# A hybrid decoder block on one core: 160 gathered tokens and 352 dense ones instead of 128 and 384

## The chip, the core and the metric

The program runs on one core of one Trainium2 chip. The metric is the device time of one execution in microseconds. A Trainium2 core has a matrix engine (TensorE, PE in the rows, with its weight loads as PEld), a vector engine (DVE), a scalar engine (ACT), a general engine (GpSimd, POOL) and a queue engine (SyncE, SP). Each engine runs its own instructions in order; 16 DMA engines move data between memory and the on-chip buffer of 128 partitions.

## What is computed

512 tokens of 2048 channels and 16 learned tokens ahead of them go through two mixers side by side (a convolution and a gated linear attention), a residual, and a mixture of 16384 tiny experts ("PEER"). The change is in the last part alone:

```python
def _peer(xn, wq, k1, k2, U, V):            # 8 heads, 128 keys, top 16
    q = (xn @ wq).reshape(B, L, 8, 256)
    s1 = einsum('blhd,hnd->blhn', q[..., :128], k1)
    s2 = einsum('blhd,hnd->blhn', q[..., 128:], k2)
    v1, i1 = top_k(s1, 16); v2, i2 = top_k(s2, 16)
    cand, cidx = v1[..., :, None] + v2[..., None, :], i1[..., :, None] * 128 + i2[..., None, :]
    top_s, pos = top_k(cand, 16)
    idx, gate = cidx[pos], softmax(top_s)   # 8 * 16 = 128 experts of each token
    h = gelu(einsum('thkd,td->thk', U[idx], x))
    return einsum('thk,thkd->td', gate * h, V[idx])
...
h = h + mixed @ w_out
h = h + _peer(rmsnorm(h, norm2_g), ...)
return rmsnorm(h, normf_g)[:, 16:]
```

U and V have 16384 rows of 2048 fp32 numbers, 8 KB a row. Each token uses 128 of them.

## The kernel before

The experts are computed in two ways. The first 128 tokens are **gathered**: a token lies on each partition, and for each of its 128 slots one indirect DMA (`_gather`, L711, issued by POOL at L713) brings 128 rows, one a partition, 1 MB, into a buffer `rows`, of which there are two. For the rows of U, DVE multiplies them with the token and sums (L731, result in a column of `gw`); for those of V, it adds them, times a weight, to `ytok` (L746). That is 256 gathers, the 128 of U first. The other 384 tokens (`TD`) are **dense**: TensorE multiplies them with all 16384 rows of U and V, each fp32 number split into a high and a low part, in three products (L87, L89, L91 for U; L873 to L875 for V), and the gate of an expert that a token did not choose is zero. A weight tile of 1 MB is loaded by SP into `raw` (two buffers), ACT writes its high half `whi` (L68) and DVE the low half `wlo` (L71), in two halves of 1024 columns, of which three buffers each exist.

After the mixers (the first 2050 us of the span) the program runs in these stages:

- the choice (`_select`, to 2309 us): queries, scores, top 16, with the tokens' rows (`_token_rows`, `xtok`, L702) and the dense tokens' normed columns (`_dense_row`, tile `dnh`, four buffers, loaded by POOL's queue at L578). DVE has nearly all of it. In this stage POOL also computes `wlo`.
- B, 2310 to 2850 us: the tiles of U from 8 to 60 (128 experts a tile, 48 matmuls of 384 columns, `_up_tile`), whose results go to memory (`hlag`). Beside each tile stands a step of `_gate_steps`, which makes the dense gates by one-hot products, 8 tokens at a time (48 such steps): DVE compares (`b` L774, `a` L776), POOL and ACT multiply (`ag`), TensorE multiplies (`pg`), ACT and DVE write them out (`stage`, L795). One gather follows each tile.
- D, 2877 to 3373 us: groups 0 to 6 of the second product. A group is 1024 experts; it has four quarters of the output's channels, each two tiles of V and 96 matmuls. After each quarter `gather(2)`. `_w_piece` loads gates (`gt`, L842) and hidden values (`gel`, L848) through POOL's queue and multiplies them on DVE (L851, L509).
- E, 3373 to 4446 us: groups 7 to 14, each quarter followed by two more tiles of U for the next group, and the gathers that are left (147) shared evenly over 96 places, three in a quarter. A quarter here is 192 matmuls and four weight tiles.
- the last group, 4446 to 4521 us, in which `_Final` finishes the gathered tokens: it transposes `ytok`, adds the residual `hg` (L971), squares and sums (L974), scales and stores them, while the last experts of the others run; then 19 us for the norm of the dense tokens.

The list of gathers is one queue (`gsteps`); `gather(n)` takes the next n. Each engine's order is fixed by a scheduler when the program is built: what stands under `high_priority` (weights, `_w_piece`, sums into `yT` at L882) goes ahead, and a gather is issued no earlier than the last `wlo` emitted before it. The gather's DVE step stands in DVE's one queue among the `wlo` that TensorE needs next.

Of the kernel before, what the change touches and what calls it, by code (L numbers as in the profile page):

```python
# [698 lines left out]
def _token_rows(g, sp):
    """The normed rows of the first TG tokens, token on partition."""  # L700
    nc = g.nc
    nc.gpsimd.tensor_tensor(g.xtok.rearrange("p (c t) -> p c t", t=TG), _bf(g.x2h[:, :, :TG]), _bf(g.x2l[:, :, :TG]), op=OP.add)  # L702
    for c in range(4):
        cs = slice(c * 512, (c + 1) * 512)
        ps = g.p2.tile([P, 512], F32, tag="ps2", name="ps2")
        for j in range(4):
            _transpose(nc, ps[:, j * P:(j + 1) * P], g.xtok[:, c * 512 + j * P:c * 512 + (j + 1) * P], g.ident)
        nc.scalar.activation(g.xtok[:, cs], ps, AF.Copy, scale=g.rc[:, :1])


def _gather(g, rows, src, col):  # L711
# [7 lines left out]
def _gather_steps(g):  # L719
    """The experts of the first TG tokens, row by row: one closure per gathered set of rows."""  # L720
    nc, a = g.nc, g.a
    st = Ctx()

    def up(s):
        def f():
            if s == 0:
                st.h = g.gp.tile([P, SLOTS], F32, name="ghd")
                st.w = g.gp.tile([P, SLOTS], F32, name="gw")
            rows = g.rp.tile([P, D], F32, tag="rows", name="rows", bufs=2)
            _gather(g, rows, a["un"], s)  # L730
            nc.vector.scalar_tensor_tensor(rows, rows, 1.0, g.xtok, op0=OP.mult, op1=OP.mult, accum_out=st.h[:, s:s + 1])  # L731
            if s % TOPK == TOPK - 1:
                hs = slice(s + 1 - TOPK, s + 1)
                nc.scalar.activation(st.w[:, hs], st.h[:, hs], AF.Gelu)
                nc.vector.tensor_tensor(st.w[:, hs], st.w[:, hs], g.gate[:, 0, hs], op=OP.mult)
        return f

    def down(s):
        def f():
            rows = g.rp.tile([P, D], F32, tag="rows", name="rows", bufs=2)  # L740
            _gather(g, rows, a["vn"], s)
            if s == 0:
                g.ytok = g.gp.tile([P, D], F32, tag="xtok", name="ytok", bufs=1)
# [409 lines left out]
```

## Time and profile before

| | us |
|---|---|
| median of 3 runs | 4539.19 |
| lowest, highest | 4538.23, 4542.43 |
| span of the profiled execution | 4539.7 |
| TensorE busy | 4405.1 (97%) |
| DVE busy | 3228.6 (71%) |
| ACT busy | 1588.5 (35%) |
| POOL busy | 1005.2 (22%) |

The profiled execution is 0.5 us from the median of the runs, and its span starts with the first instruction and ends with the last; nothing else of it has a row. The page's shares are means over stages with quite different limits, so the rows below go by stage.

### The profile page before, as it was taken

Reading aid. Unit: us, or ns where it says so; the run is one execution under the profiler, and the core shown is the slowest. Engines: PE = TensorE matmul, PEld = TensorE weight load, DVE = VectorE, ACT = ScalarE, POOL = GpSimd, SP = SyncE. Lnnn points to the kernel's source line nnn. Section 1 sums busy time; section 2 is a strip of 40 time slices with the busy share of each in tenths; the row PEclk is TensorE's granted clock in tenths of the full one; section 3 lists DMA queues with packets and bytes.
Section 4 is the critical chain, followed back from the end, with each engine's and each line's share of the span. In section 5 each row is a group of like instructions: output and inputs, shape, how many; then the busy total and the mean of one; then the engine's idle time right before and its main releaser. Section 6 shows DMA issues by size and latency. Waiting matters only on the chain.

```text
span 4539.7 us, 61723 instructions
## 1 busy us (share of the span) xinstructions
PE 4405.1 (97%) x24991; PEld 4094.5 (90%) x24991; DVE 3228.6 (71%) x4355; ACT 1588.5 (35%) x2309; POOL 1005.2 (22%) x644
## 2 busy tenths in 40 slices
PE   8999999999999999998899999999999999999998
PEld 8888899998888888877799998999999999999997
DVE  8999965555553434339999999577776767767776
ACT  4222223334362222232246666322233233332323
POOL 2222200000000000023345555223222222212120
PEclk9999999999999999999999999999999999999999
DMA  4222222222443644432257777877777777777774
GB/s 151 98 100 106 108 87 74 75 75 89 156 149 124 220 141 145 141 120 97 93 207 281 288 260 279 300 291 274 290 273 276 277 285 281 280 279 287 282 294 147
DMA packets 164926, 882.45 MB, mean 194 GB/s; under 512 B 19360, under 2 KB 32224, under 8 KB 76704
## 3 DMA queue, kind: packets, MB, share of 16 engines
q1 hardware_dynamic: 64736, 459.04, 27.5%
q0 software_dynamic: 56352, 335.57, 20.9%
q10 hardware_dynamic: 43552, 83.89, 5.4%
q8 instruction: 195, 3.19, 0.3%
q14 instruction: 91, 0.75, 0.0%
HBM read 807.13 MB, written 71.30 MB: 194 GB/s over the span
## 4 chain that ended last, share of the span: by engine, by line
PE 72%; DVE 16%; issue 6%; DMA 3%; ACT 2%; POOL 1%; ACTq 0%; DVEq 0%; POOLq 0%; SPq 0%
PE mm L91 10%; PE mm L89 10%; PE mm L87 10%; DVE cacc L174 8%; PE pu L87 7%; PE pu L91 7%; PE pu L89 7%; PE pv L875 6%; PE pv L873 6%; PE pv L874 6%; DVE wlo L71 3%; DMA rows<-un,eidx 1%; DMA gel<-hlag 1%; DVE rows L731 1%; DVE stage L795 1%
## 5 line engine op out<-in xcount | busy, mean ns | idle before, releaser
L68 ACT CAST whi<-raw 128x1024 fp32r<-128x1024 f32 x866 | 904.5, 1048 | 2176.7 <-PE mm L89 804.0
L71 DVE TENSOR_TENSOR wlo<-raw,whi 128x1024 fp32r<-128x1024 f32 (+1 forms) x773 | 1024.8, 1328 | 662.4 <-ACT whi L68 659.4
L91 PE MATMUL mm<-xh,wlo 128*128 128x264 f32 (+2 forms) x2720 | 728.4, 322 | 23.4 <-POOL wlo L71 19.6
L87 PE MATMUL mm<-xl,whi 128*128 128x264 f32 (+2 forms) x2720 | 735.4, 325 | 11.0 <-DVE xl L141 11.0
L89 PE MATMUL mm<-xh,whi 128*128 128x264 f32 (+2 forms) x2720 | 727.4, 322 | 0.0
L875 PE MATMUL pv<-wh,wlo 128*128 128x384 f32 x2048 | 689.0, 336 | 19.5 <-DVE wlo L71 19.5
L87 PE MATMUL pu<-dl,whi 128*128 128x384 f32 x2048 | 695.8, 340 | 10.4 <-ACT whi L68 10.4
L91 PE MATMUL pu<-dh,wlo 128*128 128x384 f32 x2048 | 695.1, 339 | 3.3 <-DVE wlo L71 1.9
L89 PE MATMUL pu<-dh,whi 128*128 128x384 f32 x2048 | 695.2, 339 | 0.0
L873 PE MATMUL pv<-wl,whi 128*128 128x384 f32 x2048 | 687.7, 336 | 1.6 <-ACT whi L68 0.6
L874 PE MATMUL pv<-wh,whi 128*128 128x384 f32 x2048 | 687.3, 336 | 0.0
L91 PEld LDWEIGHTS mm<-xh,wlo 128*128 128x128 f32 (+1 forms) x2720 | 450.8, 188 | 69.2 <-POOL wlo L71 25.2
L87 PEld LDWEIGHTS mm<-xl,whi 128*128 128x128 f32 (+1 forms) x2720 | 452.9, 188 | 57.6 <-DVE xl L141 11.6
L89 PEld LDWEIGHTS mm<-xh,whi 128*128 128x128 f32 (+1 forms) x2720 | 450.5, 188 | 42.6 <-issue 4.2
L174 DVE SCALAR_TENSOR_TENSOR cacc<-hg,cw,cacc 128x512 f32<-128x512 f32 x480 | 413.4, 861 | 15.2
L875 PEld LDWEIGHTS pv<-wh,wlo 128*128 128x128 f32 x2048 | 386.8, 189 | 23.1 <-DVE wlo L71 22.8
L87 PEld LDWEIGHTS pu<-dl,whi 128*128 128x128 f32 x2048 | 387.3, 189 | 10.8 <-ACT whi L68 10.8
L91 PEld LDWEIGHTS pu<-dh,wlo 128*128 128x128 f32 x2048 | 387.2, 189 | 4.1 <-DVE wlo L71 2.2
L873 PEld LDWEIGHTS pv<-wl,whi 128*128 128x128 f32 x2048 | 386.8, 189 | 2.7 <-ACT whi L68 0.9
L89 PEld LDWEIGHTS pu<-dh,whi 128*128 128x128 f32 x2048 | 387.4, 189 | 0.0
L874 PEld LDWEIGHTS pv<-wh,whi 128*128 128x128 f32 x2048 | 386.8, 189 | 0.0
L746 DVE SCALAR_TENSOR_TENSOR ytok<-rows,gw,ytok 128x2048 f32<-128x2048 f32 x127 | 298.1, 2347 | 51.6 <-DMA rows<-vn,eidx 51.0
(281 smaller groups left out, 5676.7 us busy)
## 6 DMA issues: line engine op xcount, KB each, us to landing
raw<-ut SPq DMA_DIRECT2D x128, 1024.0 KB, 6.6
raw<-vt SPq DMA_DIRECT2D x128, 1024.0 KB, 7.9
raw<-wp SPq DMA_DIRECT2D x111, 1024.0 KB, 4.8
gd<-stage ACTq DMA_DIRECT2D x48, 512.0 KB, 7.2
gt<-gd POOLq DMA_DIRECT2D x32, 768.0 KB, 6.6
raw<-wco SPq DMA_DIRECT2D x16, 1024.0 KB, 5.7
raw<-wgo SPq DMA_DIRECT2D x16, 1024.0 KB, 4.7
raw<-wo SPq DMA_DIRECT2D x16, 1024.0 KB, 4.8
```

What stands on the lines that cost most here:

```text
L68: nc.scalar.copy(hi, raw[:, s * h:(s + 1) * h])
L71: g.last = eng.tensor_tensor(lo, raw[:, s * h:(s + 1) * h], _bf(hi), op=OP.subtract).ins
L87: nc.tensor.matmul(ps, wh, xl[:, k, cs], start=k == 0, stop=False)
L89: nc.tensor.matmul(ps, wh, xh[:, k, cs], start=False, stop=False)
L91: nc.tensor.matmul(ps, wl, xh[:, k, cs], start=False, stop=k == KT - 1)
L174: nc.vector.scalar_tensor_tensor(acc, hg[:, w:w + SEQ], cw[:, w:w + 1], acc, op0=OP.mult, op1=OP.add)
L731: nc.vector.scalar_tensor_tensor(rows, rows, 1.0, g.xtok, op0=OP.mult, op1=OP.mult, accum_out=st.h[:, s:s + 1])
L746: nc.vector.scalar_tensor_tensor(g.ytok, rows, st.w[:, s:s + 1], g.ytok, op0=OP.mult, op1=OP.add)
L795: nc.vector.tensor_tensor(so, so, pr[:, 1], op=OP.add)
L873: nc.tensor.matmul(o, hi[:, c:c + P], wl[:, j], start=first, stop=False)
L874: nc.tensor.matmul(o, hi[:, c:c + P], wh[:, j], start=False, stop=False)
L875: nc.tensor.matmul(o, lo[:, c:c + P], wh[:, j], start=False, stop=last)
```

## The change

Thirty-two more tokens, the first of the second block of 128, become gathered ones. Each takes four partitions, and each of these holds 32 of its 128 slots: partition 32 j + t has the slots 32 j to 32 j + 31 of token 128 + t. So 32 gathers of U and 32 of V serve them, of 128 rows each like the others, and the list of gathers has 320 entries instead of 256: the old 128 and 128, then 32 of U and 32 of V. The dense width `TD` falls from 384 to 352 columns everywhere, the steps of `_gate_steps` from 48 to 44, and the blocks of gates in memory from 12 to 11.

Around it: `_spread` copies indices and gates into the new layout by small DVE copies; `_token_rows` makes a second set of token rows (`xtokx`) with one POOL operation, 17 transposes and 5 ACT copies; `dnh` has two buffers instead of four; `gather(2)` in D becomes `gather(2 + q % 2)`, so that a group takes 10 instead of 8; what is left for E is 197 instead of 147, shared by the same rule. In `_Final` the sum over the four partitions of a token is a product of `ytokx` with a matrix `sel` (16 fp32 matmuls into one tile), and the tiles `hg`, `zg` and the store are 160 columns wide. The two `rows` buffers stay two; they are sized by `hg` and `zg`.

```diff
-TG = 128
+TB0 = 128
+EX = 32
+JX = P // EX
+TG = TB0 + EX
 TD = SEQ - TG
...
-    h = sp.tile([P, TD], F32, name="dnh", bufs=4)
+    h = sp.tile([P, TD], F32, name="dnh", bufs=2)
...
+    x1 = sp.tile([P, EX], F32, tag="tku", name="x1", bufs=1)
+    x2 = sp.tile([P, EX], F32, tag="tkq", name="x2", bufs=1)
+    _spread(g, x1, g.i1)
+    _spread(g, x2, g.i2)
+    nc.vector.scalar_tensor_tensor(x1, x1, float(NK), x2, op0=OP.mult, op1=OP.add)
+    nc.vector.tensor_copy(g.eidxx, x1)
...
+    nc.gpsimd.tensor_tensor(g.xtokx.rearrange("p (c j t) -> p c j t", j=JX, t=EX), _bf(g.x2h[:, :, None, ts]).to_broadcast(sx), _bf(g.x2l[:, :, None, ts]).to_broadcast(sx), op=OP.add)
...
+def _spread(g, out, src):
+
+    for j in range(JX):
+        g.nc.vector.tensor_copy(out[j * EX:(j + 1) * EX], src[:EX, 1, j * EX:(j + 1) * EX])
...
-    return [up(s) for s in range(SLOTS)] + [down(s) for s in range(SLOTS)]
...
+        return [up(s) for s in range(n)] + [down(s) for s in range(n)]
+
+    return (block(SLOTS, g.eidx, lambda hs: g.gate[:, 0, hs], g.xtok, "xtok", lambda y: setattr(g, "ytok", y))
+            + block(EX, g.eidxx, lambda hs: g.gatex[:, hs], g.xtokx, "xtokx", lambda y: setattr(g, "ytokx", y)))
...
-                    gather(2)
+                    gather(2 + q % 2)
...
+        sel = g.gp.tile([P, EX], F32, name="sel")
+        nc.vector.tensor_reduce(sel, g.ident.rearrange("p (j t) -> p t j", t=EX), axis=AX.X, op=OP.add)
+        pt = g.pv.tile([P, 512], F32, tag="pv", name="pt")
+        for ct in range(KT):
+            nc.tensor.matmul(pt[:, ct * EX:(ct + 1) * EX], g.ytokx[:, ct * P:(ct + 1) * P], sel, start=True, stop=True)
+        nc.vector.tensor_tensor(zg[:, :, P:], pt.rearrange("p (c t) -> p c t", t=EX), hg[:, :, P:], op=OP.add)
```

The order in three places. First, DVE in a quarter of E, around the sums into `yT` (L882 before, L914 after). Before:

```order
L71 TENSOR_TENSOR wlo<-raw,whi 128x1024
L746 SCALAR_TENSOR_TENSOR ytok<-rows,gw,ytok 128x2048 x2
L71 TENSOR_TENSOR wlo<-raw,whi 128x1024 x2
L746 SCALAR_TENSOR_TENSOR ytok<-rows,gw,ytok 128x2048
L882 TENSOR_TENSOR yT<-yT,pv 128x384 x4
L71 TENSOR_TENSOR wlo<-raw,whi 128x1024 x2
L746 SCALAR_TENSOR_TENSOR ytok<-rows,gw,ytok 128x2048 x2
L71 TENSOR_TENSOR wlo<-raw,whi 128x1024
L851 TENSOR_TENSOR gel<-gel,gt 128x384
```

The same place in the changed kernel (L74 is the old L71, L775 the old L746):

```order
L74 TENSOR_TENSOR wlo<-raw,whi 128x1024
L775 SCALAR_TENSOR_TENSOR yxtok<-rows,gwxtok,yxtok 128x2048 x2
L74 TENSOR_TENSOR wlo<-raw,whi 128x1024 x2
L775 SCALAR_TENSOR_TENSOR yxtok<-rows,gwxtok,yxtok 128x2048
L914 TENSOR_TENSOR yT<-yT,pv 128x352 x4
L74 TENSOR_TENSOR wlo<-raw,whi 128x1024
L775 SCALAR_TENSOR_TENSOR yxtok<-rows,gwxtok,yxtok 128x2048
L74 TENSOR_TENSOR wlo<-raw,whi 128x1024
L775 SCALAR_TENSOR_TENSOR yxtok<-rows,gwxtok,yxtok 128x2048
L74 TENSOR_TENSOR wlo<-raw,whi 128x1024
L883 TENSOR_TENSOR gel<-gel,gt 128x352
L775 SCALAR_TENSOR_TENSOR yxtok<-rows,gwxtok,yxtok 128x2048
```

From the sums to the first `gel` there stand two steps of gathered rows in either; a third follows at once in the changed kernel, and between two such steps there is often one `wlo` where there were two.

Second, POOL's queue in D, over one turn of two quarters. Before:

```order
L713 DMA rows<-un,eidx 128x2048
L848 DMA gel_24340<-hlag 128x384
L842 DMA gt<-gd 128x12x128
L848 DMA gel_24619<-hlag 128x384
L713 DMA rows<-un,eidx 128x2048
L842 DMA gt<-gd 128x12x128
L713 DMA rows<-un,eidx 128x2048 x6
```

And in the changed kernel:

```order
L738 DMA rows<-un,eidx 128x2048
L880 DMA gel_24249<-hlag 128x352
L880 DMA gel_24254<-hlag 128x352
L880 DMA gel_24259<-hlag 128x352
L874 DMA gt<-gd 128x11x128
L880 DMA gel_24543<-hlag 128x352
L874 DMA gt<-gd 128x11x128
L738 DMA rows<-un,eidx 128x2048 x8
```

Eight gathers follow one another where there were six, with the loads of the next pieces behind them on the same queue.

Third, DVE where the last group begins and the gathered tokens are finished. Before:

```order
L746 SCALAR_TENSOR_TENSOR ytok<-rows,gw,ytok 128x2048
L71 TENSOR_TENSOR wlo<-raw,whi 128x1024
L971 TENSOR_TENSOR zg<-pt,hg 128x512
L71 TENSOR_TENSOR wlo<-raw,whi 128x1024
L851 TENSOR_TENSOR gel<-gel,gt 128x384
L971 TENSOR_TENSOR zg<-pt,hg 128x512
```

And in the changed kernel:

```order
L775 SCALAR_TENSOR_TENSOR yxtokx<-rows,gwxtokx,yxtokx 128x2048
L883 TENSOR_TENSOR gel<-gel,gt 128x352
L74 TENSOR_TENSOR wlo<-raw,whi 128x1024
L512 TENSOR_TENSOR wl<-gel,wh 128x352
L1041 TENSOR_TENSOR yT<-yT,hx 128x1408
L1004 TENSOR_TENSOR zg<-pt,hg 128x4x128 x4
L1010 TENSOR_TENSOR zg<-pt,hg 128x16x32
L1013 TENSOR_REDUCE gst<-hg 128x160
L74 TENSOR_TENSOR wlo<-raw,whi 128x1024 x2
```

The five additions into `zg` and the sum of squares now stand in one run ahead of two `wlo`. The last place of E takes three gathers instead of two.

## Rows read from the trace of the kernel before

**Rows 1.** Busy time by stage: bounds, length, engines, clock, DMA share, GB/s.
```profile
core 0: us, PE busy (x) PEld busy (x) DVE busy (x) ACT busy (x) POOL busy (x), PEclk, DMA share, GB/s
2050.00:2310.00 260.00, 228.31 (x1089) 197.58 (x1087) 259.42 (x886) 76.70 (x137) 103.53 (x53) 0.94 0.29 100
2310.00:2850.00 540.00, 513.43 (x2927) 501.84 (x2928) 521.70 (x506) 338.65 (x741) 288.06 (x103) 0.99 0.76 275
2877.00:3373.00 496.00, 475.92 (x2687) 472.07 (x2686) 361.26 (x444) 149.49 (x192) 146.86 (x129) 0.98 0.78 285
3373.00:4446.00 1073.00, 1073.00 (x6144) 1073.00 (x6143) 765.46 (x684) 323.87 (x384) 228.49 (x164) 1.00 0.77 282
4446.00:4521.00 75.00, 71.39 (x411) 69.53 (x410) 44.98 (x53) 30.60 (x50) 5.80 (x2) 1.00 0.31 108
```
**Rows 2.** Same view, short stretches: 512 columns, 384 columns, two with busy DMA.
```profile
1850.00:1900.00 50.00, 50.00 (x216) 40.25 (x215) 18.85 (x21) 14.06 (x17) 2.16 (x4) 1.00 0.40 135
3450.00:3500.00 50.00, 50.00 (x288) 50.00 (x287) 35.50 (x38) 13.94 (x16) 9.57 (x8) 1.00 0.73 270
...
2800.00:2850.00 50.00, 47.98 (x273) 47.44 (x272) 43.84 (x46) 26.91 (x52) 17.64 (x9) 0.97 0.88 317
...
2810.00:2820.00 10.00, 10.00 (x60) 9.87 (x60) 10.00 (x12) 7.25 (x17) 4.92 (x2) 1.00 1.02 394
```
**Rows 3.** The choice: a DVE group, POOL's wait (us, times, longest), `xtok`.
```profile
L655 DVE SCALAR_TENSOR_TENSOR tkg<-i,i 128x16 f32<-128x16 f32 x8 | 1.9, 233 | 0.0
...
POOL dnh L578 <- DVE dl L509: 34.2, 5, 16.7
...
2014.58 5.07 POOL L702 TENSOR_TENSOR xtok<-x2h,x2l 128x2048 f32<-128x2048 f32 x1
```
**Rows 4.** DVE's groups in B: busy us, mean ns, idle before.
```profile
L795 DVE TENSOR_TENSOR stage<-stage,pg 128x256 f32<-128x256 f32 x192 | 115.5, 680 | 0.0
L774 DVE TENSOR_TENSOR b<-iota,i2T 128x1024 fp32r<-128x1024 f32 x48 | 67.4, 1404 | 0.0
L776 DVE TENSOR_TENSOR a<-iota,i1T 128x1024 f32<-128x1024 f32 x48 | 58.8, 1225 | 0.0
```
**Rows 5.** D: waits of PE and DVE, then the gathers' landing.
```profile
PE pv L875 <- DVE wlo L71: 19.5, 8, 5.1
...
DVE rows L731 <- DMA rows<-un,eidx: 36.7, 7, 7.6
...
DMA to landing us min/median/max: 6.2/8.2/12.7
```
**Rows 6.** E: DVE's two largest groups, POOL's wait for buffers, gathers' landing.
```profile
L71 DVE TENSOR_TENSOR wlo<-raw,whi 128x1024 fp32r<-128x1024 f32 x255 | 310.8, 1222 | 225.9 <-ACT whi L68 225.9
L746 DVE SCALAR_TENSOR_TENSOR ytok<-rows,gw,ytok 128x2048 f32<-128x2048 f32 x127 | 298.1, 2347 | 51.6 <-DMA rows<-vn,eidx 51.0
...
POOL rows L713 <- DVE ytok L746: 571.0, 103, 15.9
...
DMA to landing us min/median/max: 5.5/7.2/9.3
```
**Rows 7.** Timeline in E: buffer freed, next gather, its step (start, us).
```profile
3826.24 2.35 DVE L746 SCALAR_TENSOR_TENSOR ytok<-rows,gw,ytok 128x2048 f32<-128x2048 f32 x1 [1.91 <-DMA rows<-vn,eidx]
...
3828.86 0.99 POOL L713 DMA_INDIRECT rows<-vn,eidx  x1 [6.04 <-DMA rows<-vn,eidx]
...
3837.22 2.35 DVE L746 SCALAR_TENSOR_TENSOR ytok<-rows,gw,ytok 128x2048 f32<-128x2048 f32 x1 [2.24 <-DMA rows<-vn,eidx]
```
**Rows 8.** DMA in E: q0 gathers, q1 weights (packets, MB, share); all D.
```profile
q0 software_dynamic: 24767, 167.43, 43.4%
q1 hardware_dynamic: 18432, 134.23, 33.6%
...
DMA packets 23246, 141.23 MB, mean 285 GB/s; under 512 B 2989, under 2 KB 3117, under 8 KB 8986
```
**Rows 9.** The start of the last group: PE's wait, DVE's timeline.
```profile
PE pt L219 <- DVE ytok L746: 1.4, 1, 1.4
...
4445.95 2.35 DVE L746 SCALAR_TENSOR_TENSOR ytok<-rows,gw,ytok 128x2048 f32<-128x2048 f32 x1 [1.60 <-DMA rows<-vn,eidx]
...
4456.18 3.78 DVE L974 TENSOR_REDUCE gst<-hg 128x128 f32<-128x2048 f32 x1 [1.99 <-ACT hg L972]
4459.89 1.20 DVE L71 TENSOR_TENSOR wlo<-raw,whi 128x1024 fp32r<-128x1024 f32 x1
```

More of the change, by code (lines that the diff above doesn't have):

```diff
@@ L701, in _token_rows, with _gather @@
     nc = g.nc
[L702 to L711, printed above, removed]
+    sx = [P, KT, JX, EX]
+    ts = slice(TB0, TG)
+    nc.gpsimd.tensor_tensor(g.xtok.rearrange("p (c t) -> p c t", t=P), _bf(g.x2h[:, :, :P]), _bf(g.x2l[:, :, :P]), op=OP.add)
+    nc.gpsimd.tensor_tensor(g.xtokx.rearrange("p (c j t) -> p c j t", j=JX, t=EX), _bf(g.x2h[:, :, None, ts]).to_broadcast(sx), _bf(g.x2l[:, :, None, ts]).to_broadcast(sx), op=OP.add)
+    rx = sp.tile([P, JX, EX], F32, tag="tkx", name="rx", bufs=1)
+    nc.vector.tensor_copy(rx, g.rs2[:, None, ts].to_broadcast([P, JX, EX]))
+    pt = g.p2.tile([P, 512], F32, tag="ps2", name="ps2")
+    _transpose(nc, pt[:, :P], rx.rearrange("p j t -> p (j t)"), g.ident)
+    rcx = sp.tile([P, 1], F32, name="rcx")
+    nc.scalar.copy(rcx, pt[:, :1])
+    for x, r in ((g.xtok, g.rc[:, :1]), (g.xtokx, rcx)):
+        for c in range(4):
+            cs = slice(c * 512, (c + 1) * 512)
+            ps = g.p2.tile([P, 512], F32, tag="ps2", name="ps2")
+            for j in range(4):
+                _transpose(nc, ps[:, j * P:(j + 1) * P], x[:, c * 512 + j * P:c * 512 + (j + 1) * P], g.ident)
+            nc.scalar.activation(x[:, cs], ps, AF.Copy, scale=r)
+def _spread(g, out, src):
+    for j in range(JX):
+        g.nc.vector.tensor_copy(out[j * EX:(j + 1) * EX], src[:EX, 1, j * EX:(j + 1) * EX])
+def _gather(g, rows, src, idx, col):
     nc = g.nc
@@ L721, in _gather_steps @@
     nc, a = g.nc, g.a
[L722 to L743, printed above, removed]
-                nc.vector.tensor_scalar(g.ytok, rows, st.w[:, 0:1], None, op0=OP.mult)
-            else:
-                nc.vector.scalar_tensor_tensor(g.ytok, rows, st.w[:, s:s + 1], g.ytok, op0=OP.mult, op1=OP.add)
-        return f
-    return [up(s) for s in range(SLOTS)] + [down(s) for s in range(SLOTS)]
+    def block(n, idx, gate, x, tag, keep):
+        st = Ctx()
+        def up(s):
+            def f():
+                if s == 0:
+                    st.h = g.gp.tile([P, n], F32, name="gh" + tag)
+                    st.w = g.gp.tile([P, n], F32, name="gw" + tag)
+                rows = g.rp.tile([P, D], F32, tag="rows", name="rows", bufs=2)
+                _gather(g, rows, a["un"], idx, s)
+                nc.vector.scalar_tensor_tensor(rows, rows, 1.0, x, op0=OP.mult, op1=OP.mult, accum_out=st.h[:, s:s + 1])
+                if s % TOPK == TOPK - 1:
+                    hs = slice(s + 1 - TOPK, s + 1)
+                    nc.scalar.activation(st.w[:, hs], st.h[:, hs], AF.Gelu)
+                    nc.vector.tensor_tensor(st.w[:, hs], st.w[:, hs], gate(hs), op=OP.mult)
+            return f
+        def down(s):
+            def f():
+                rows = g.rp.tile([P, D], F32, tag="rows", name="rows", bufs=2)
+                _gather(g, rows, a["vn"], idx, s)
+                if s == 0:
+                    st.y = g.gp.tile([P, D], F32, tag=tag, name="y" + tag, bufs=1)
+                    keep(st.y)
+                    nc.vector.tensor_scalar(st.y, rows, st.w[:, 0:1], None, op0=OP.mult)
+                else:
+                    nc.vector.scalar_tensor_tensor(st.y, rows, st.w[:, s:s + 1], st.y, op0=OP.mult, op1=OP.add)
+            return f
+        return [up(s) for s in range(n)] + [down(s) for s in range(n)]
@@ L764, in head @@
             ps = g.pv.tile([P, 512], F32, tag="pv", name="pg")
-            for b in range(TD // P):
-                _transpose(nc, ps[:, b * P:(b + 1) * P], src[:, TG // P + b], g.ident)
-            nc.scalar.copy(dst, ps[:, :TD])
+            for b in range(3):
+                _transpose(nc, ps[:, b * P:(b + 1) * P], src[:, 1 + b], g.ident)
+            nc.scalar.copy(dst, ps[:, EX:3 * P])
         nc.scalar.copy(st.gh, st.g)
@@ L891, in _peer @@
             _softmax(g, sp)
+            _spread(g, g.gatex, g.gate)
     g.lopool = ()
@@ L1078, in _body @@
             g.eidx = gp.tile([P, SLOTS], I32, name="eidx")
+            g.eidxx = gp.tile([P, EX], I32, name="eidxx")
+            g.gatex = gp.tile([P, EX], F32, name="gatex")
             g.xtok = gp.tile([P, D], F32, tag="xtok", name="xtok", bufs=1)
+            g.xtokx = gp.tile([P, D], F32, tag="xtokx", name="xtokx", bufs=1)
             sp = _select(g)
```

6 lines of the change are left out of this document (3 added, 3 removed).

## The prediction

> **What bounds the kernel now.** I read the busy times by stage first, since the page's means mix stages with different limits. [rows 1] In E TensorE is busy for the whole 1073 us, 6144 matmuls of 384 columns, 174.6 ns each, at the full clock, while DVE has 71%. So E costs what its matmuls cost. In B DVE is busy for 521.7 of 540 us and TensorE for 513.4: both near full, DVE first. In the choice DVE has 259.4 of 260 us. In D TensorE works 475.9 of 496 us, and what ends its waits is `wlo`, DVE's low half of a weight: 19.5 us in 8 waits. [rows 5] DVE is late there because it stood in its queue behind a step of gathered rows that had not landed (36.7 us, 7 waits). In E DVE waits 51.0 us for gathers too, but no wait reaches TensorE. [rows 6]
>
> Next the gathers as a ring. There are two `rows` buffers: POOL waits 571.0 us in E for DVE to free one. [rows 6] One turn can be read from the timeline: a buffer is freed at 3828.59 (3826.24 + 2.35), the next gather is issued at 3828.86, its DVE step starts at 3837.22 and ends at 3839.57: 10.98 us. [rows 7] With the median landing of 7.2 us it is 0.27 + 7.2 + 2.35 = 9.8 us. [rows 6, 7] Two buffers give a gather every 4.9 us. E wants 147 gathers in 32 quarters of 33.5 us, 4.6 in each, one in 7.3 us: the ring has slack now.
>
> **The change part by part.**
>
> Price of a column. A fully busy 50 us hold 216 matmuls of 512 columns (231.5 ns) or 288 of 384 (173.6 ns): 0.452 ns a column, so 32 columns fewer save 14.5 ns, and one matmul takes about 160 ns. [rows 2] All 12288 dense matmuls together would give back 178 us. This is what there is to gain; the rest is what stage lets it through.
>
> The choice. DVE is full, so each copy of `_spread`, the index arithmetic and the copy of the norm counts: some 15 small ones, none dearer than the 233 ns of a 128x16 step: at most 3.5 us; the eight per cent narrower `dnh` steps give about 1.5 back. [rows 3] The second `xtokx` costs POOL what the first did, 5.07 us, ahead of its `wlo` halves: 0 to 5 us. [rows 3] `dnh` with two buffers: POOL already waits 34.2 us for the four to come free, with `wlo` queued behind on POOL and TensorE behind that. [rows 3] With two, these waits begin a pair earlier. As DVE has a backlog all through the stage, waiting moves rather than adds: 0, or up to 12 us if DVE ever runs dry. Together +3 (0 to +12).
>
> B. DVE decides, and four of 48 gate steps fall away: `b` and `a` cost 67.4 + 58.8 = 126.2 us, a twelfth is 10.5; `stage` 115.5 us, a twelfth is 9.6. [rows 4] The `wlo` and the 53 gathers stay. So -20, where TensorE alone would give 2544 x 14.5 ns = 37. Range -30 to -14, as TensorE now and then is the later one. The three tiles of U after B: 144 matmuls, -2.
>
> D. 2688 matmuls x 14.5 ns = -39 us with the waits as they are. But a group takes 10 gathers instead of 8 in less time (496 - 39 = 457 us for seven groups, 65 each): 14 more, 14.7 MB, onto 141.2 MB less a twelfth of gates and hidden values (about 2): 154 MB, at 457 us 337 GB/s where it is 285 now. [rows 1, 8] The landing here is 8.2 us in the median and up to 12.7 [rows 5], and the order shows eight gathers in a row with the loads of the next piece behind them: the existing chain (late rows, DVE held, `wlo` late) gets links. From all of the gain lost and half of the present 36.7 us of late rows added again (+18) to the full -39; I take -15, since two of ten gathers are new and each turn lost costs about what a long wait costs now (7.6 us, less the slack of the weights). [rows 5]
>
> E. At TensorE's pace a quarter of 192 matmuls takes 30.7 us (33.5 now), -89 over 32 quarters. Three other things want time in it.
> - DVE: 765.5 us in 32 quarters are 23.9 now; 1.56 more steps of gathered rows at 2.35 make 27.6 of 30.7, 90%; not the bound by itself, but with less room to let a `wlo` wait. [rows 1, 6]
> - The ring: 197 gathers in 32 quarters are 6.16 a quarter, one in 4.98 us. The turn at the median landing allows 4.9, the turn in the timeline 5.49 (33.8 us a quarter). [rows 6, 7]
> - DMA: 6.16 + 4 tiles of 1.049 MB and 0.35 for gates are 11.0 MB, in 30.7 us 359 GB/s; by the shares now (43.4% for 167.4 MB, 33.6% for 134.2) a quarter would keep the 16 engines busy for 30.4 of the 30.7 us. [rows 8] The busiest 50 us of these stages have 317 GB/s at a share of 0.88, the busiest 10 us 394 at 1.02. [rows 2]
>
> So the traffic cannot stay as quick as it is. The landing will rise from 7.2 towards D's 8.2; I take 8.0 [rows 5, 6], a turn of 10.6, 5.3 us a gather, 32.6 us a quarter. A step of rows that is late holds the `wlo` behind it, and TensorE loses what the ring lacks. Saving 33.5 - 32.6 = 0.9 x 32 = -29, between -89 (ring quick enough) and the two ends of the rivals below.
>
> The Trainium skill, "DMA: Bandwidth & Descriptors", Specifications, gives about 358 GB/s as the limit of one core's share of the memory. By that rule E would sit just at the limit, 11.0 MB in 30.7 us. The row with 394 GB/s in 10 us does not bear a hard wall there out. [rows 2]
>
> The last group. 384 matmuls give -5.6. The last place of E takes three gathers, so the third lands a turn later (about +9 us) than the last does now, when TensorE waits 1.4 us for it; then come the load of `hg`, five additions, a square and a sum over 160 columns (3.78 us now, 4.7 then) ahead of two `wlo`. [rows 9] I take it that this eats the saving: 0 (-5 to +12). The tail: 352 instead of 384 columns, -1.
>
> Sum: 4539.7 + 3 - 20 - 2 - 15 - 29 + 0 - 1 = **4475.7**; the profiled execution is within 0.5 us of the median, so I say **4476**.
>
> **The rivals.**
>
> 1. The ring keeps up. If the landing stays at 7.2, a gather takes 4.9 us and E runs at 30.7 us a quarter: -89, and D keeps -30 or so. 4539.7 + 3 - 20 - 2 - 30 - 89 - 1 = 4401. For it: DVE's 51.0 us of waits in E hurt nothing today, and narrower matmuls do not make the loads longer. [rows 6] Against: the share of 0.99 that this asks of the DMA engines. [rows 1, 8]
> 2. The DMA engines are the ceiling, somewhat over the 0.88 of the busiest 50 us. At 0.92 a quarter takes 30.4 / 0.92 = 33.0 us; at 317 GB/s 34.7. [rows 2, 8] E gives -16 to +38, D -5; 4499 to 4553, so mostly about nothing. For it: the whole gain then goes into moving 67 MB more. Against: the share inside short stretches reaches 1.
> 3. Slower, by the ring. It decides where the turn passes 11.2 us: 5.6 us a gather, 34.5 us a quarter, +32 in E, which eats the other gains; that is a landing of 8.6 us with two buffers. At 9.0, below the 9.3 that single gathers of E and the 12.7 that those of D take today [rows 5, 6], it is 11.62 / 2 x 6.16 = 35.8 us, +73 in E, and with D at 0 the total is 4539.7 + 3 - 22 + 73 - 1 = 4593. For it: all 32 quarters lie in it, and each late gather also delays the next. Against: it needs the median to go where only the slowest are now.
> 4. The choice swallows the gain: if two `dnh` buffers hold POOL's `wlo` back in every pair, eight pairs at 4 us are +30 and the total is 4505. [rows 3] Little speaks for it, as DVE has work waiting.
>
> **How the numbers follow.** The forecast (E between 31.5 and 33.0 us a quarter; 4440 to 4500) has 0.45, rival 1 (4390 to 4440) 0.25, rival 2 0.16, rival 3 0.11, rival 4 0.03. A difference of 0.2%, 9 us, is about what a measurement of this kernel can tell from no change. Faster by more than that is all of the forecast, rival 1 and rival 4, and a small part of rival 2: 0.76. Within it falls most of rival 2: 0.10. Slower: rival 3 and the far end of rival 2: 0.14. The range reaches from rival 1's sum (with a little of its lower half left out) to 4550, where rival 3 begins.
>
> **What would show it.** In the changed profile: 50 us of E with more than 300 matmuls if TensorE sets the pace (312 at 160 ns), and 290 to 300 if the ring does; TensorE's waits in E, none now, should be on `wlo` with DVE's waits on gathered rows before them, above 51.0 us by far; the landing in E between 7.5 and 8.5 us; a DMA share of 0.90 to 0.96 there; B shorter by about 20 us with DVE still nearly full; a wait on the last gather of 5 us or more at the start of the last group. I am wrong in mechanism if TensorE waits in E for `raw` loads (the weights' traffic, not the ring), or if the waits come where no row is late.

## The result: slower by 0.66%

The changed kernel takes 4563.84 us (median of 4 runs, 4556.98 to 4571.06) against 4538.71 for the kernel before (4 runs): a ratio of 1.0066, 95% interval 1.0050 to 1.0082. Forecast were 4476 us, in a range from near rival 1's sum (4401) up to 4550. The profiled execution has a span of 4558.0 us, 18.3 more than before.

The borders of the stages (the first matmul of the tile that opens each) show where it went:

| stage | before, us | after, us | difference | predicted |
|---|---|---|---|---|
| up to tile 8 of U (mixers, choice) | 2308.6 | 2312.1 | +3.5 | +3 |
| B, tiles 8 to 60 | 542.9 | 527.3 | -15.6 | -20 |
| tiles 61 to 63 | 25.4 | 27.7 | +2.3 | -2 |
| D | 496.6 | 472.1 | -24.5 | -15 |
| E without its last quarter | 1039.7 | 1086.2 | +46.5 | -29 |
| the last quarter of E | 36.9 | 49.8 | +12.9 | (in E) |
| last group and tail | 89.6 | 82.8 | -6.8 | -1 |

So the forecast holds to some 10 us everywhere except in E, and there it has the wrong sign. These are two single executions: B, which the twelve runs below leave as the changed kernel has it, took 506 to 527 us in them, so a difference of 10 or 20 us in one stage is no more than a hint. The busy times by stage, to be read against [rows 1] (bounds, length, busy us and instructions of each engine, granted clock, DMA share, GB/s):

```profile
core 0: us, PE busy (x) PEld busy (x) DVE busy (x) ACT busy (x) POOL busy (x), PEclk, DMA share, GB/s
...
2312.00:2839.00 527.00, 475.71 (x2905) 462.08 (x2904) 514.17 (x499) 320.64 (x694) 272.69 (x99) 0.98 0.77 274
...
2867.00:3339.00 472.00, 442.99 (x2687) 437.79 (x2688) 381.45 (x473) 147.90 (x194) 162.74 (x144) 0.97 0.90 324
3339.00:4475.00 1136.00, 1030.89 (x6195) 1009.93 (x6193) 868.70 (x759) 316.55 (x389) 318.96 (x215) 0.97 0.84 314
```

In E TensorE was busy all the time before; now it is not, although its matmuls got shorter. Its waits in E, and DVE's (engine, tile and line that waited, what ended the wait, us in total, times, longest):

```profile
PE pv L907 <- DVE wlo L74: 52.8, 30, 3.6
PE pu L94 <- DVE wlo L74: 44.6, 29, 4.4
PE pt L1009 <- DVE yxtokx L775: 7.2, 1, 7.2
...
DVE yxtok L775 <- DMA rows<-vn,eidx: 156.7, 69, 4.3
DVE rows L759 <- DMA rows<-un,eidxx: 38.8, 17, 4.9
DVE yxtokx L775 <- DMA rows<-vn,eidxx: 30.1, 17, 4.2
...
DVE wlo L74 <- ACT whi L71: 9.5, 22, 0.6
```

TensorE had no wait in E before, but for 1.4 us at its end [rows 9]; now it waits 97.4 us in 59 times for `wlo`, and 7.2 us at the end for the last rows. DVE stands at gathered rows (it has nothing else to do in its order until they land) for 236.4 us (these rows and three small ones) where it stood for 56.7 (51.0 of them in [rows 6], the rest at the last rows of U). And what DVE waited for most before, ACT's `whi` (225.9 us [rows 6], the slack of a DVE that is ahead), is down to 9.5 us. DVE's work and its standing at rows are 868.7 + 236.4 = 1105 of the 1136 us: its one queue is full, with work or with standing.

One such place in the timeline of DVE and POOL (start, us):

```profile
3817.36 2.35 DVE L775 SCALAR_TENSOR_TENSOR yxtok<-rows,gwxtok,yxtok 128x2048 f32<-128x2048 f32 x1
...
3823.39 1.22 DVE L74 TENSOR_TENSOR wlo<-raw,whi 128x1024 fp32r<-128x1024 f32 x1
3824.53 0.52 DVE L883 TENSOR_TENSOR gel<-gel,gt 128x352 f32<-128x352 f32 x1
3828.49 2.35 DVE L775 SCALAR_TENSOR_TENSOR yxtok<-rows,gwxtok,yxtok 128x2048 f32<-128x2048 f32 x1 [3.44 <-DMA rows<-vn,eidx]
3830.76 1.22 DVE L74 TENSOR_TENSOR wlo<-raw,whi 128x1024 fp32r<-128x1024 f32 x1
...
3819.98 1.73 POOL L738 DMA_INDIRECT rows<-vn,eidx  x1 [4.13 <-DVE yxtok L775]
...
3832.03 0.43 PE L907 MATMUL pv<-wh,wlo 128*128 128x352 f32 x1 [2.81 <-DVE wlo L74]
```

The step at 3817.36 frees a buffer, POOL issues the next gather into it at 3819.98, and its step begins at 3828.49, 8.5 us later. DVE has reached that step 3.44 us before and stands; the `wlo` behind it starts at 3830.76, and TensorE, which needs it, stands for 2.81 us until 3832.03.

### The profile page after: what moved, and what is told of

It is laid out like the page before. It is cut to its first block, busy times and chain, and to the rows that moved or that the text cites. A ratio compares the mean times of both kernels' runs of the same rounds, so it can differ in the third digit from the quotient of the medians.

```text
span 4558.0 us, 62049 instructions
## 1 busy us (share of the span) xinstructions
PE 4281.0 (94%) x25008; PEld 3946.5 (87%) x25008; DVE 3340.3 (73%) x4446; ACT 1558.8 (34%) x2268; POOL 1102.5 (24%) x705
## 4 chain that ended last, share of the span: by engine, by line
PE 30%; DVE 24%; issue 23%; DMA 18%; POOL 2%; ACT 1%; POOLq 0%; ACTq 0%; DVEq 0%; SPq 0%
DMA rows<-vn,eidx 11%; DVE cacc L177 7%; PE mm L94 7%; PE mm L92 6%; PE mm L90 6%; DVE wlo L74 4%; DMA rows<-vn,eidxx 3%; DVE rows L759 2%; DMA rows<-un,eidx 2%; PE pu L94 2%; PE pu L90 2%; PE pu L92 2%; POOL rows L738 2%; DVE stage L827 1%; DMA gel<-hlag 1%
## 5 line engine op out<-in xcount | busy, mean ns | idle before, releaser
L71 ACT CAST whi<-raw 128x1024 fp32r<-128x1024 f32 x866 | 900.2, 1046 | 2008.1 <-PE mm L92 804.4
L74 DVE TENSOR_TENSOR wlo<-raw,whi 128x1024 fp32r<-128x1024 f32 (+1 forms) x773 | 1030.5, 1339 | 402.7 <-ACT whi L71 399.8
L907 PE MATMUL pv<-wh,wlo 128*128 128x352 f32 x2048 | 674.5, 329 | 82.6 <-DVE wlo L74 82.3
L94 PE MATMUL pu<-dh,wlo 128*128 128x352 f32 x2048 | 673.4, 329 | 55.2 <-DVE wlo L74 52.6
L90 PE MATMUL pu<-dl,whi 128*128 128x352 f32 x2048 | 671.0, 328 | 12.2 <-ACT whi L71 12.2
L905 PE MATMUL pv<-wl,whi 128*128 128x352 f32 x2048 | 669.6, 327 | 4.7 <-DVE wl L512 4.7
L906 PE MATMUL pv<-wh,whi 128*128 128x352 f32 x2048 | 668.5, 326 | 0.0
L92 PE MATMUL pu<-dh,whi 128*128 128x352 f32 x2048 | 666.8, 326 | 0.0
L90 PEld LDWEIGHTS mm<-xl,whi 128*128 128x128 f32 (+1 forms) x2720 | 453.7, 188 | 57.3 <-DVE xl L144 11.2
L775 DVE SCALAR_TENSOR_TENSOR yxtok<-rows,gwxtok,yxtok 128x2048 f32<-128x2048 f32 x127 | 298.5, 2350 | 157.0 <-DMA rows<-vn,eidx 156.7
```

The costliest lines, as they stand in the source:

```text
L71: nc.scalar.copy(hi, raw[:, s * h:(s + 1) * h])
L74: g.last = eng.tensor_tensor(lo, raw[:, s * h:(s + 1) * h], _bf(hi), op=OP.subtract).ins
L90: nc.tensor.matmul(ps, wh, xl[:, k, cs], start=k == 0, stop=False)
L92: nc.tensor.matmul(ps, wh, xh[:, k, cs], start=False, stop=False)
L94: nc.tensor.matmul(ps, wl, xh[:, k, cs], start=False, stop=k == KT - 1)
L775: nc.vector.scalar_tensor_tensor(st.y, rows, st.w[:, s:s + 1], st.y, op0=OP.mult, op1=OP.add)
```

## The experiments

The stage E of each run, from the first matmul of group 7 to that of the last group, with DVE's work, its standing at gathered rows (all rows of that wait summed), TensorE's waits for `wlo`, and the time of the whole kernel. E and what stands beside it come from one profiled execution each. The total is a median of four runs, but of one run for e2, e3, e5, e7, e8 and e10, where differences of 10 or 20 us are not to be read closely:

| kernel | rows buffers | gathers in E | E, us | DVE work | DVE at rows | PE at wlo | total, us |
|---|---|---|---|---|---|---|---|
| before (384 wide) | 2 | 147 | 1077 | 768 | 57 | 0 | 4539 |
| changed | 2 | 197 | 1136 | 869 | 236 | 97 | 4564 |
| e3_narrow_alone | 2 | 133 | 986 | 734 | 41 | 2 | 4392 |
| e4_three_in_D | 2 | 183 | 1101 | 847 | 212 | 77 | 4569 |
| e5_two_in_D | 2 | 211 | 1188 | 900 | 260 | 130 | 4607 |
| e2_shared_weights | 2 | 197 | 1106 | 870 | 210 | 79 | 4523 |
| e7_half_step | 2 | 197 | 1078 | 708 | 291 | 61 | 4477 |
| e8_half_rows | 2 | 197 | 1065 | 871 | 163 | 50 | 4480 |
| e10_four_places | 2 | 197 | 1115 | 875 | 210 | 85 | 4527 |
| e1_three_rows | 3 | 197 | 1007 | 871 | 28 | 7 | 4402 |
| e6_early_end | 3 | 197 | 1005 | 871 | 49 | 13 | 4394 |
| e9_two_in_D | 3 | 211 | 1029 | 896 | 76 | 30 | 4425 |
| e11_three_rows_four_places | 3 | 197 | 987 | 870 | 42 | 3 | 4387 |
| e12_four_places_three_in_D | 3 | 183 | 983 | 844 | 3 | 1 | 4407 |

**Three buffers instead of two.** `rows` gets 8 KB and three buffers after stage B; the finish of the gathered tokens goes in two halves of the channels to make room.

```diff
-            rows = g.rp.tile([P, D], F32, tag="rows", name="rows", bufs=2)
+            rows = g.rp.tile([P, D], F32, tag="rows", name="rows", bufs=g.rbufs)   # 2 in B, 3 after
...
-        hg = g.rp.tile([P, KT, TG], F32, tag="rows", name="hg", bufs=2)
+        hgs = [g.rp.tile([P, KT // 2, TG], F32, tag="rows", name="hg", bufs=3) for _ in range(2)]
```

> The changed kernel with three buffers of 8 KB for gathered rows in stages D and E instead of two (and the finish of the gathered tokens in two halves of the channels, so that it fits). Stage E of the changed kernel takes 1136 us; there DVE waits 237 us for gathered rows, the mean turn of a buffer is 11.5 us (0.3 to the issue, 7.3 to the last packet, 1.5 until DVE begins, 2.35 its step) and TensorE waits 97 us for wlo. Ring theory (two buffers are too few for a turn of this length; the DMA engines have room): DVE's waits for rows fall below 60 us, E falls to 985-1030 us, near TensorE's pace of 30.7 us a quarter, total 4420-4460. DMA theory (the 16 engines cannot move more than now, 314 GB/s at a share of 0.84): the landing grows by what the third buffer gives, E stays above 1100 us and the total above 4530. DVE theory (27 us of work a quarter and its fixed order are the limit, whatever the rows do): waits for rows shrink, but wlo is as late as now, E 1090-1140.

Measured: 4401.51 us, ratio to before 0.970 (0.9683 to 0.9717). E in this run, and DVE's two largest waits there:

```profile
3321.00:4328.00 1007.00, 991.50 (x6192) 989.58 (x6191) 870.68 (x763) 319.71 (x390) 360.17 (x215) 0.99 0.93 354
...
DVE wlo L74 <- ACT whi L71: 73.8, 72, 4.1
DVE yxtok L775 <- DMA rows<-vn,eidx: 16.0, 16, 2.3
```

DVE does the same work, the gathers are the same, and more bytes move in a microsecond; the standing at rows went from 236.4 to 28.1 us, and E with it. The DMA theory falls: 354 GB/s at a share of 0.93 where 314 at 0.84 had looked like a limit. The DVE theory falls: the same 870 us of work fit into 1007.

**The narrower columns alone**, and **weights loaded once for two uses.**

```diff
-    return (block(SLOTS, g.eidx, ..., g.xtok, "xtok", ...)
-            + block(EX, g.eidxx, ..., g.xtokx, "xtokx", ...))
+    g.ytokx = g.xtokx
+    return block(SLOTS, g.eidx, ..., g.xtok, "xtok", ...)
```

> The changed kernel without the 64 gathers of the 32 additional tokens (their experts' sum is left out; their token rows, the reduction and the columns of the output stay), so the dense part is 352 wide and the list has 256 gathers, 133 in stage E. All theories: this is the price of the columns alone. E at TensorE's pace, 30.7 us a quarter, 985-995 us, no wait of TensorE there; D 455-475 us; total 4395-4420. If E is longer than 1020 us, a matmul of 352 columns costs more than 160 ns or something besides the gathers holds it.

Measured: 4392.22 us, E 986 us, all but 2 of it TensorE at work:

```profile
3323.00:4309.00 986.00, 983.86 (x6192) 983.55 (x6191) 734.15 (x665) 320.06 (x386) 227.38 (x151) 1.00 0.81 294
```

6192 matmuls (48 of them small ones of the finish) in 983.9 us are 158.9 ns each; the prediction had 160. So the price of a column was right. The 64 gathers on two buffers cost the difference to the changed kernel, 172 us, 150 of them in E.

```diff
-        if not parts:
+        if not parts and not old:      # old: the tile that the one before has loaded
             nc.sync.dma_start(raw, src)
```

> The changed kernel; in stage E each loaded weight tile serves twice (the second tile of V of a quarter and the second tile of U use the bytes of the first), so half of the weight loads of E are left out and the results of E with them; all casts, subtractions, matmuls and gathers stay. The traffic of a quarter falls from 11.0 to 8.9 MB. DMA theory (traffic sets the pace): E falls by up to 19%, from 1136 to 985-1000 us. Ring theory with a landing that is mostly issue and fixed latency (3.55 us from issue to the first packet, 3.8 of transfer): only the transfer part shrinks, by 0.5 to 1 us of a turn of 11.5, E 1040-1100 us, and TensorE still waits for wlo behind late rows. DVE theory: 1120-1140.

Measured: 4522.67 us, E 1106 us, the DMA share down to 0.72:

```profile
3331.00:4437.00 1106.00, 1022.17 (x6194) 1007.53 (x6193) 869.98 (x765) 317.75 (x390) 366.38 (x216) 0.97 0.72 262
```

A fifth less traffic gives 30 us, a little less than the least that the ring theory allowed. By the DMA packets of the gathers in E, the last packet comes 6.8 us after the issue here and 7.3 in the changed kernel: without half of the weight loads the landing is some 0.5 us shorter. An earlier `raw` has little to give: DVE waited 9.5 us for `whi` in the changed kernel and waits 9.9 here.

**Fewer and more gathers in E**, by `gather(3)` or `gather(2)` after every quarter of D instead of 2 and 3 by turns.

> The changed kernel with three gathers after every quarter of stage D (12 a group instead of 10), so 84 in D and 183 in E instead of 70 and 197. Ring theory: a gather costs E 5.77 us (1136/197), so E falls by about 80 us to 1055, and D, whose groups take 67 us for 10 gathers (at 5.5 us a gather 12 need 66), rises by 0 to 25 us: total 4485-4515, faster than the kernel before. DMA theory: the bytes only move from one busy stage to another, E gains about 47 us and D loses 25-47: total 4545-4565. DVE theory: 14 steps of 2.3 us move, E gains about 32 us, D loses up to 32: total 4550-4565.

Measured: 4569.42 us, ratio to before 1.0072 (1.0043 to 1.0101), no better than the changed kernel. D, then E:

```profile
2858.00:3391.00 533.00, 464.64 (x2688) 452.86 (x2689) 406.16 (x486) 147.22 (x195) 179.22 (x157) 0.94 0.84 311
...
3391.00:4492.00 1101.00, 1019.60 (x6195) 1002.84 (x6194) 846.64 (x749) 317.07 (x388) 300.08 (x203) 0.98 0.83 313
```

This miss taught most. E gave back 35 us, not the 80 that the ring theory had, and D lost 61 us (472 to 533). A gather less in E is worth 2.35 us of DVE's work and the 1.2 us that DVE stands at an average one (236.4 / 197), 3.5 us: 49 for 14, more than the 35 seen, but nearer than 80. From that came an account that could be tested: work and standing add in DVE's queue.

D shows the same account. With twelve gathers a group DVE stands there at rows for 93.2 us (38.5 with ten), and its waits for ACT's `whi`, the sign of a DVE that is ahead, are gone (21.1 with ten, 43.8 with the eight of the next run):

```profile
DVE rows L759 <- DMA rows<-un,eidx: 83.7, 42, 6.4
...
DVE wlo L74 <- ACT whi L71: 0.8, 1, 0.8
```

> The changed kernel (two buffers) with two gathers after every quarter of D, so 56 in D and 211 in stage E instead of 70 and 197. It tests an account formed from the runs so far: in E, DVE's one queue is full (862 us of work and 230 us of standing blocked at gathered rows out of 1126), and both add; a gather costs it 2.35 us of work and 1.2 us of standing, 3.5 together, 14 more cost 49 us. Additive account: E 1170-1200 us. Turn account (E is gathers times half a turn of 11.5 us, whatever DVE does): 211 x 5.77 = 1217, E 1205-1230 us. In both D falls by 10-25 us from 472; total 4570-4600 by the first, 4605-4635 by the second.

Measured: E 1188 us (+52, where 49 was foretold), total 4607.19, some us over the upper end: D, expected 10 to 25 us shorter, stayed at 472.

```profile
3336.00:4524.00 1188.00, 1047.44 (x6192) 1024.85 (x6190) 900.07 (x789) 316.18 (x390) 334.11 (x228) 0.96 0.83 312
```

**Shorter work or shorter landing.** If DVE's load alone were the cause, a shorter transfer could not help.

```diff
-  scalar_tensor_tensor(st.y, rows, st.w[:, s:s + 1], st.y, ...)
+  scalar_tensor_tensor(st.y[:, :D // 2], rows[:, :D // 2], st.w[:, s:s + 1], st.y[:, :D // 2], ...)   # e7
...
+  rows, src = rows[:, :D // 2], src.rearrange("n (h d) -> (n h) d", h=2)   # e8, in _gather for V; the DVE step (not shown) reads this half twice
```

> The changed kernel (two buffers); the DVE step of the rows of V works on the first 1024 of their 2048 channels, so half of the gathered sums is left out; each gather still moves 1 MB. The step falls from 2.35 to about 1.2 us, a turn from 11.5 to 10.3 us, DVE's work in a quarter from 27.1 to 21. Ring theory (what matters is the turn, whatever part of it is shortened): E 1020-1070 us instead of 1136. DVE theory (its load matters): E 985-1010, with DVE's waits for rows as long as now or longer.

> The changed kernel (two buffers); each gather of V moves rows of 1024 channels (0.5 MB), and the DVE step reads these twice, so it is as long as now and stands in the same order; the gathered sums are other ones. The transfer (3.8 us from the first to the last packet) falls to about 2, a turn from 11.5 to 9.6 us; DVE's work stays at 27 us a quarter. Ring theory: E 990-1040 us, DVE's waits for rows below 120 us (237 now). DVE theory: E 1100-1136, wlo late as now. DMA theory as before is not at issue here, since both traffic and turn fall.

Measured: E 1078 us with the half step (4477.12 in all), 1065 with the half rows (4480.33); the busy times in E of the half step

```profile
3315.00:4393.00 1078.00, 1011.48 (x6194) 996.44 (x6193) 708.29 (x766) 316.22 (x390) 304.68 (x216) 0.99 0.87 331
```

and of the half rows

```profile
3331.00:4396.00 1065.00, 1005.55 (x6196) 991.59 (x6194) 870.93 (x764) 317.48 (x389) 339.92 (x215) 0.99 0.71 257
```

Both help about alike. In the first DVE's work falls by 160 us and its standing rises by 55: what DVE does not work, it partly stands, and it also waits 51.3 us for `whi` (9.5 before), so its queue is not full here and the sum of work and standing (999 of 1078 us) does not give E; a turn of the ring, two buffers' worth of E's time a gather, is 10.9 us for 11.5. In the second its work is unchanged and the standing falls by 73. Neither reaches the bounds that either theory had alone (1020 to 1070 and 990 to 1040 for the ring); work and ring act together. Each is a single run.

**Spacing.** Four places for gathers in a quarter of E, one after each weight tile, instead of three.

```diff
-                    share = [... for j in range(3)]
+                    share = [... for j in range(4)]      # the first of them between the two tiles of V
```

> The changed kernel (two buffers, the same 197 gathers in stage E, the same work), with four places for them in a quarter instead of three: one after each weight tile, so that steps of gathered rows stand more evenly between DVE's other work. With three places a quarter takes 35.0 us, and in the run with 14 fewer gathers in E it was still 34.2. Spacing theory (a turn of 11 us with two buffers hurts where three steps stand close together, since the third can't land in time): E 32-33.5 us a quarter, 1030-1080 us, TensorE's waits for wlo below 60 us (97 now). Mean-rate theory (only gathers per time and turn count): 34.5-35.5 us a quarter, E 1110-1140.

Measured: E 1115 us, 4526.52 in all (a single run): 21 us, not the 56 to 106 of the spacing theory; it fits the 1110 to 1140 of the mean-rate theory.

```profile
3327.00:4442.00 1115.00, 1026.03 (x6191) 1011.36 (x6190) 874.63 (x767) 317.83 (x389) 320.54 (x216) 0.97 0.86 320
```

**Towards a better kernel.** On top of three buffers: no gather in the last quarter of E; then 56 gathers in D; then four places a quarter; then 84 gathers in D.

> Three buffers as before, and the gathers of stage E shared over its first 93 places, so that none stands in the last quarter, whose length with three buffers was 55.8 us against 30.5 for the others (TensorE waits 8.8 us for the last rows, then 7.0 us of the 32 fp32 passes that sum the four partitions of a token, 3.2 us of transposes, and waits for wlo behind the sums of squares on DVE). Ring theory: E stays at 30.5-30.7 us a quarter (6.35 gathers a quarter instead of 6.16), the last quarter falls to 41-46 us, total 4380-4395. If DVE is full (27.5 us of work in 30.5), the other quarters grow to 31-32 us and the total is 4400-4430.

Measured: 4394.39 us, ratio 0.9673 (0.9648 to 0.9699). The last quarter fell from 55.8 to 37.2 us, the others rose from 30.7 to 31.2: the intervals of this kernel and of three buffers alone overlap. The total fits the ring theory, the 31.2 us the other.

> Three buffers, no gather in the last quarter of E, and two gathers after every quarter of D instead of two and three by turns: 56 in D and 211 in E over 93 places, 6.8 a quarter. Ring theory: E has room up to the rate of three buffers (a turn of about 13 us with the landing of 8.7 us seen with three, 4.3 us a gather, 7.1 a quarter), so E stays near 30.7 us a quarter, D loses 5-15 us of its waits, total 4370-4390. If DVE is full (28.6 us of work in 30.5): E 31.5-32.5 us a quarter, total 4395-4430.

Measured: 4425.30 us, ratio 0.9749 (0.9725 to 0.9773); E 1029 us, 32.0 a quarter without the last, and D 449 for 452: the case of a full DVE, not of a ring with room.

> Three buffers, no gather in the last quarter of E, and four places in each other quarter, one after each weight tile. Spacing theory: the waits for wlo that three buffers and three places left (12.7 us, and with them stretches at half clock) go, E falls from 1004 to 985-995 us, total 4375-4388. Mean-rate theory: the same as with three places, 4386-4404.

Measured: 4387.33 us, ratio 0.9666 (0.9641 to 0.9692), the lowest median of all. E is at TensorE's pace:

```profile
3317.00:4304.00 987.00, 984.06 (x6190) 983.16 (x6189) 869.55 (x761) 320.31 (x389) 345.17 (x215) 1.00 0.94 361
```

Its total lies at the upper end of what the spacing theory said and also in what the other said, so this run does not decide between them. In E the 64 gathers cost nothing any more: 987 us, where the kernel that leaves them out takes 986.

> The same with three gathers after every quarter of D (84 there, 183 in E over 124 places, 5.9 a quarter). If the DMA engines are what is left (three kernels with 11.0 to 11.7 MB a quarter all moved 356-358 GB/s at a share of 0.94), E gets 0.3 MB a quarter less, 10.7 MB in 30.5 us are 351 GB/s, and E is at TensorE's pace, 980-985 us, but D, at 63-65 us a group with 10 gathers, wants 12: 154 + 14.7 MB in 358 GB/s are 472 us, 15-20 more than now. Total 4385-4405, no gain over the run without it. If the engines have room, D stays near 455 and the total is 4370-4380.

Measured: 4407.23 us, ratio 0.9708 (0.9687 to 0.9728): E 983 us, D 478 us, a group in 68.

```profile
2860.00:3337.00 477.00, 446.31 (x2691) 437.87 (x2691) 406.53 (x486) 144.94 (x194) 197.59 (x156) 0.98 0.93 351
```

D had no room for the gathers, as the first of the two cases said (whose range ended at 4405, 2 us lower). Whether that is the DMA engines or DVE (406.5 us of work, 34.5 at rows and 29.8 at `gel`, in 477, with 5.9 at `whi`), this run leaves open.

## Why the prediction was wrong, step by step

- The price of a column: right. 158.9 ns measured for 160.
- The choice: +3.5 for +3. The start of tile 8 moves by some 6 us among the runs, so this hardly tests it, and the two `dnh` buffers were not tried apart from the rest.
- B: -15.6 for -20, and -16 to -37 over all the runs; DVE is again the fuller one (514.2 of 527 us).
- D: -24.5 for -15, within its bounds.
- **E is the step that failed**: the turn of the ring was too short by a term that the sum put at nothing. The prediction took "a turn of 10.6", that is 0.27 to the issue, 8.0 of landing and 2.35 of work, as if DVE began each step the moment that its row lands. Measured are 11.5 us. In the mean of E's 196 gathers these are 0.3 to the issue, 7.3 to the last packet, 0.4 until DVE can know of it, 1.1 us by which DVE is late, and 2.35 of work; without the 1.1 two buffers would have allowed 32 us a quarter. DVE stood waiting at 108 of the rows; the other 88 had landed and waited for DVE, whose queue had other work first, for 2.6 us after the last packet on average.

  The prediction set DVE's work (27.6 of 30.7 us), the ring (32.6) and the DMA engines (30.4) side by side and let the longest decide. But DVE's steps and its standing lie in one queue in order: 868.7 us of work and 236.4 of standing, 27.1 + 7.4 = 34.5 us a quarter, of the 35.5 that E's 1136 us give each of 32. While DVE stands it does no `wlo`, and once the row is there the work that has piled up makes the next step late too.
- The landing within that turn: "The landing will rise from 7.2 towards D's 8.2; I take 8.0". The number came out, for another reason than the one given. By the packets, the median gather's last packet came 7.0 us after its issue before and 7.7 now, and with 0.4 to the signal that is 7.4 and 8.1 (the 7.2 of [rows 6] rests on the 17 of the gathers that the view has a landing for). But the traffic did not slow the transfer: from the first packet to the last it took 3.9 us in the mean before and 3.8 now. What grew is the time from the issue to the first packet, 3.0 to 3.7 us in the median, and as much longer POOL was busy with the issue itself (0.99 to 1.73 us, below). So that this term fits is luck.
- Rival 3 ("Slower, by the ring. It decides where the turn passes 11.2 us") named the place and the turn, with a chance of 0.11; its reason, "a landing of 8.6 us", was not the one. What spoke against it in the text, "it needs the median to go where only the slowest are now", overlooked that DVE's lateness lengthens a turn without any change in the landing.
- Rival 2, the DMA engines as the ceiling: refuted by e1 and e11, which moved 354 and 361 GB/s through the same stage. The Trainium skill, "DMA: Bandwidth & Descriptors", Specifications, puts one core's share of the memory at about 358 GB/s. The 361 GB/s over 987 us here are at that figure and slightly above. What the two-buffer kernel got (314) was no limit.
- The clock, which the sum left out of E. After some stalls the matmuls of the changed kernel follow each other in 0.29 us instead of 0.16 for some us. The stretch shown stands at the start of the last group, behind a stall of 7.2 us and the sums below; its granted clock was 0.50, that is 1.2 of 2.4 GHz (first row, with the columns as above):

```profile
4475.20:4479.00 3.80, 3.80 (x14) 3.80 (x15) 2.32 (x4) 0.00 (x0) 0.00 (x0) 0.50 0.01 3
...
4475.93 0.49 PE L907 MATMUL pv<-wh,wlo 128*128 128x352 f32 x1
4476.22 0.49 PE L905 MATMUL pv<-wl,whi 128*128 128x352 f32 x1
4476.52 0.49 PE L906 MATMUL pv<-wh,whi 128*128 128x352 f32 x1
```

TensorE was busy for 1030.9 us in E for work that took 983.9 in e3, which has the same matmuls. The granted clock is 0.973 in the mean of E where e3 has 1.00: half of the full one in 61 of the 1136 us. By that about 30 of the 47 us are the lower clock, an estimate, or 0.3 us for each us of waiting for `wlo`; the rest is not assigned.
- The last group: a wait of "5 us or more" for the last rows was foretold, and it is 7.2 us. Overlooked were the 16 fp32 matmuls with `sel`, which the sum gave no price. Here they are in the changed kernel, and in e11, where no stall stands before them:

```profile
4468.35 7.04 PE L1009 MATMUL pt<-sel,yxtokx 128*128 128x32 f32 x32 [7.16 <-DVE yxtokx L775]
...
4297.77 3.65 PE L1012 MATMUL pt<-sel,yxtokx 128*128 128x32 f32 x32
```

They run as 32 passes and hold TensorE for 7.0 us here, at a granted clock of 0.50, and for 3.65 in e11 at 1.00. In the eight profiles with a wait of TensorE just before them they take 6.6 to 7.0 us, in the five without one 3.7. 7.0 us and a wait longer by 5.8 (7.2 for 1.4) are nearly the 12.9 by which the last quarter of E grew. The last group itself was 5.4 us shorter, as its narrower columns say (5.6).
- Tiles 61 to 63: +2.3 for -2, too little to follow up.
- The signs that the prediction named: TensorE's waits came on `wlo` behind late rows, as foretold, and not on `raw`. The DMA share in E was 0.84, below the 0.90 to 0.96 foretold, and 50 us of E hold some 270 matmuls (6144 in 1136 us), fewer than the 290 to 300 of a ring alone.

What stays open: why eight gathers a group cost D no less than ten with two buffers (472 us both), although DVE waits longer for `whi` then (43.8 us for 21.1); why POOL's issue of a gather takes longer in the changed kernel; and the 17 us of TensorE's busy time in E that the clock does not account for.

## What to carry to other kernels

An engine that works in order and also waits for transfers in that order has to pay for both: add its work and its standing before you compare the sum with the pace of the engine it feeds, and read the slack that it has from the waits on the other side (here `wlo` waiting for `whi`: 225.9 us before, 9.5 after). Such an engine is not always there when a row lands, so the turn of its buffers has a term for its lateness (1.1 of 11.5 us here). A change that moves work from a full engine to one with room, as here from TensorE's columns to DVE and the gathers, needs the depth of the buffers looked at in the same step: with two, it lost 0.66%; with a third, the same change gained 3.0%, and with the gathers also spread over more places and none at the end 3.3% (the intervals of these two overlap).

## What the runs showed of the hardware that was not expected

- 361 GB/s at a DMA share of 0.94, held over 987 us with TensorE, DVE and the gathers all at work.
- The 16 fp32 matmuls of 32 columns are 32 passes: 3.65 us at the full clock (e11), 0.11 us a pass, as long as a pass of a transpose of 128 columns (16 in 1.9 us); at half the clock, behind a stall, 7.04 us.
- The issue of an indirect DMA on POOL takes 0.99 or 1.73 us in the same stage, seldom more:

```profile
3806.11 0.99 POOL L738 DMA_INDIRECT rows<-vn,eidx  x1 [5.22 <-DMA rows<-vn,eidx]
3808.74 1.73 POOL L738 DMA_INDIRECT rows<-vn,eidx  x1 [1.64 <-DVE yxtok L775]
```

The first ran beside a step of gathered rows on DVE (3806.12), the second beside two `wlo` (3808.39). In the median it is 1.73 us in the changed kernel's E and 0.99 in that of the kernel before. That what runs on DVE decides it is not shown: no run varied it, and some issues beside a step of rows took 3.0 us.
